# The pool scale repeated by its load, a new order of early loads, and copies and norms exchanged at two changes of stage

## The chip, the cores and the metric

The kernel runs on one core of a Trainium2 chip. The metric is the device time of one execution in microseconds (us). Engines are named as the profile names them: PE (TensorE, matmuls), PEld (its weight loads), DVE (VectorE), ACT (ScalarE), POOL (GpSimd) and SP (SyncE, which issues most loads and stores). A name with a q (SPq, ACTq) is the engine's instruction queue, where DMAs are issued.

## The reference

A two-layer decoder trunk over 512 tokens of 1024 channels. The parts that matter here:

```python
def rms_norm(x, g):
    y = x * rsqrt(mean(x * x, axis=-1) + 1e-6)
    return y * g

def pool_mixer(h, w_pool, scale):          # layer 0
    # 4 channel groups of 256; group g: causal trailing mean over 2, 4, 8, 16 tokens, minus the token
    d = stack(diffs)                       # (B, S, 4, 256)
    y = einsum('bsgc,gcd->bsgd', d, w_pool).reshape(B, S, D)
    return y * scale                       # per output channel

x = x + rms_norm(pool_mixer(rms_norm(x, mix_pre_g[0]), pool_w[0], pool_scale[0]), mix_post_g[0])
x = x + rms_norm(conv_glu_ffn(rms_norm(x, ffn_pre_g[0]), ...), ffn_post_g[0])
# shared K/V from rms_norm(x, kv_norm_g); then layer 1:
x = x + rms_norm(sliding_window_attention(rms_norm(x, mix_pre_g[1]), K, V, sinks) @ w_o, mix_post_g[1])
x = x + rms_norm(conv_glu_ffn(rms_norm(x, ffn_pre_g[1]), ...), ffn_post_g[1])
```

`conv_glu_ffn` multiplies by `w_in` (1024 to 5632), convolves over three tokens, takes gelu(gate) * value and multiplies by `w_out` (2816 to 1024).

## The kernel before

The 512 tokens are four blocks of 128 (`x0` to `x3`, tokens on the partitions). Products of the large matmuls are split in two: each operand is a rounded high part and the remainder (`h`/`l`), and `mm3` issues three matmuls for one product (L319 high x high, L320 and L321 the mixed ones). So each operand costs a copy on ACT (the high part) and a subtraction on DVE (the low part).

The order of the work on PE, ACT, DVE and POOL is the order in which the program emits it; nothing reorders these four. SP's DMAs are placed by the tile framework, which also adds the waits: a tile with the same tag as another takes its buffer, and what writes it waits for the last access of the tile that had it. The eight PSUM banks are such buffers (`bank`), handed out in turn.

**Start.** PE first runs 13 matmuls on a constant tile (`keep_busy`, L346). x0 comes in two halves (L96). `mix_norm` (L356) squares x on ACT, takes the root on POOL and scales on DVE. `mix_pool` (L386 to 392) applies the pooling matrices `band` (its last 128 columns for block 0, the others for blocks 1 to 3) with matmuls in full precision and copies the result `d` on ACT. `mix_map` (L401) multiplies `d` by the weights `wp`. These are made by `mix_weights` (L375) on DVE: pool weights x pre-norm gain x pool scale. The scale is one row of 1024 numbers, but it is wanted on all 128 partitions: it is loaded into partition 0 of a zeroed tile (L87, L329), split into two parts (`mix_row`, L363 to L365), and repeated over the partitions by four matmuls with a matrix of ones into two PSUM banks (L371). After it come the post-norm (L281, L283), the pre-norm of the FFN (L304) and the transposes (`transpose_in`: PE L312, ACT L315, DVE L316) into `xT`, which the FFN multiplies (`u`, L319 to L321).

**Early loads.** x0, `band`'s last part, the scale row, the constants, the pool weights (1 MB), x2, a gain row, x3 and the first FFN weights go through SP's queue in that order; x1 and `band`'s first part through ACT's. Gain rows are loaded repeated over the partitions (`bcast_row`, L245). The scale row and the gain rows share a tag with two buffers ("bc").

**First FFN to attention.** `pass2` ends the FFN. Its last sums are formed as `X[3]` and `X[2]` on PE; `add`, `square_of`, `gain`, `root` and `update` (L665, L251, L687, L259/L260, L696) then make the post-norm and the new x. Blocks 2 and 3 are ready early: their pre-norm (`pre_a`: squares and root, `pre_b`: scaling) and their transposes (`to_attention`) stand between the matmuls. Blocks 0 and 1 follow after the last matmuls. Attention begins with the keys of blocks 2 and 3 (`kp`), their values (`vp`), and the transposes and keys of blocks 0 and 1.

**Attention to second FFN.** Per block b the output projection (`op`, two halves), the post-norm and the pre-norm are emitted (L1057 to L1067); the transposes of blocks 0 and 1 stand in between, those of 2 and 3 inside `start1`, which runs the first two units of `w_in` on two blocks at a time: `yield j, (b0, b1)` is unit j for blocks b0 to b1-1, with both its halves (gate and value).

**Tail.** In layer 1 `update` also stores x; the last are blocks 0 and 1.

Of the kernel before, what the change touches and what calls it, by code (L numbers as in the profile page):

```python
# [8 lines left out]
F32 = mybir.dt.float32  # L9
F32R = mybir.dt.float32r  # L10
# [5 lines left out]
P = 128  # L16
S = 512
D = 1024
# [53 lines left out]
def build(nc, tc, ctx, a, out):  # L72
# [7 lines left out]
    def bank(name):  # L80
        return ps.tile([P, 512], F32, tag="ps", name=name)
# [1 line left out]

    warm = pc.tile([P, P], F32, tag="t4", name="warm", bufs=3)
    nc.vector.memset(warm, 1.0)
    row = pc.tile([P, D], F32, tag="bc", name="row", bufs=2)
    nc.vector.memset(row, 0.0)  # L87
    x = [pc.tile([P, D], F32, tag="x", name=f"x{b}", bufs=4) for b in range(NB)]
    def new_xT(name):
        h = pc.tile([P, NB, KC, P], F32R, tag="xTh", name=f"xTh_{name}")  # L90
# [43 lines left out]
    def source(i):  # L134

        for l in range(2):
            if U_D1[l] <= i < U_D2[l]:
                p = i - U_D1[l]
                return 2048, [(0, a["ws"][W_OUT[l] + p][:, 0:512]), (512, sums[l][p][:, :])]
            if U_D2[l] <= i < U_D3[l]:  # L140
                m = i - U_D2[l]
                n = min(NP - 4 * m, 4) * 512
                return n, [(0, sums4[l][m][:, 0:n])]
            if U_D3[l] <= i < U_D3[l] + 6:
                m = i - U_D3[l]
                q = range(2 * m, min(2 * m + 2, NP))
                return len(q) * 1024, [((p % 2) * 1024, a["ws"][W_OUT[l] + p][:, 1024:2048]) for p in q]
        return 2048, [(0, a["ws"][i if i < U_D1[0] else i + W_SHIFT])]

    def load(i):  # L150
        if i in raws or i in ready or i >= N_UNITS:
            return
        r = pw.tile([P, 2048], F32, tag="raw", name=f"raw{i}", bufs=2)
        for o, src in source(i)[1]:
            nc.sync.dma_start(r[:, o : o + src.shape[1]], src)
        raws[i] = r
# [81 lines left out]
    def ahead(i, n=N_SLOTS):  # L238

        for k in range(i, i + n):  # L240
            split(k)
# [65 lines left out]
    def transpose_in(b, xn, xT, name):  # L307
        for h in range(2):
            pt = bank(f"tr_{name}{b}{h}")
            for k in range(4):  # L310
                kc = h * 4 + k
                nc.tensor.transpose(pt[:, k * P : (k + 1) * P], xn[:, kc * P : (kc + 1) * P], ident)  # L312
            hi = xT[0][:, b, h * 4 : (h + 1) * 4, :].rearrange("p k t -> p (k t)")
            lo = xT[1][:, b, h * 4 : (h + 1) * 4, :].rearrange("p k t -> p (k t)")
            nc.scalar.copy(hi, pt)  # L315
            nc.vector.tensor_tensor(lo, pt, hi.bitcast(F32), ALU.subtract)  # L316
# [9 lines left out]
    nc.scalar.dma_start(x[1], a["x"][1])  # L326
    nc.scalar.dma_start(band[:, :, : P + EDGE], a["band"][:, :, : P + EDGE])
    nc.sync.dma_start(band[:, :, P + EDGE :], a["band"][:, :, P + EDGE :])
    nc.sync.dma_start(row[0:1], a["pool_scale"])  # L329
    nc.sync.dma_start(cst[:, :C_LATE], a["cst"][:, :C_LATE])  # L330
    load(U_POOL)
    nc.sync.dma_start(x[2], a["x"][2])
    post_row = bcast_row(a["mix_post_g"][0], "mpost0")
# [6 lines left out]
    scale_row = [bank(f"scale_row{h}") for h in range(2)]  # L340
    scratch = bank("scratch")

    def keep_busy(n):
# [12 lines left out]
            nc.vector.tensor_scalar(halves(xm)[h], halves(x[b])[h], r, None, ALU.mult)  # L356
        xns[b] = xm

    parts = [pm.tile([P, D], F32R, tag=f"row{i}", name=f"row{i}") for i in range(2)]
    one = pm.tile([P, P], F32R, tag="one", name="one")  # L360

    def mix_row():
        nc.vector.tensor_copy(one, warm)  # L363
        nc.scalar.copy(parts[0], row)
        nc.vector.tensor_tensor(parts[1], row, parts[0].bitcast(F32), ALU.subtract)  # L365

    def mix_weights():

        for h in range(2):
            for i in range(2):  # L370
                nc.tensor.matmul(scale_row[h], one, parts[i][:, h * 512 : (h + 1) * 512], start=i == 0, stop=i == 1)  # L371
        pr = raws[U_POOL]
        for c in range(8):
            g = c // 2
            nc.vector.scalar_tensor_tensor(wp[:, c, :], pr[:, c * 256 : (c + 1) * 256], gain_col(0, c),  # L375
                                           scale_row[g // 2][:, (g % 2) * 256 : (g % 2 + 1) * 256], ALU.mult, ALU.mult)

    def mix_pool(b):
        d = pm.tile([P, D], F32, tag="d", name=f"d{b}", bufs=2)
# [32 lines left out]

    u0, u1 = U_IN[0], U_IN[0] + 1
    mix_norm(0)
    mix_row()
    mix_norm(1)
    d0 = mix_pool(0)
    mix_weights()
# [206 lines left out]
    def pass2(l, p2, G2, X, post_row):  # L625
# [32 lines left out]
        def soon(k):  # L658
            if k < len(todo):
                n, m = todo[k]  # L660
                split((U_D2 if n == 2 else U_D3)[l] + m)
                split2(n, m)

        def add(z, i, q):
            nc.vector.tensor_tensor(Z[z][i], Z[z][i], X[q][i], ALU.add)  # L665
# [12 lines left out]
        def square_of(z, i, q):  # L678

            b = i + (2 if z[0] == "2" else 0)  # L680
            first = b not in ss
            if first:
                ss[b] = new_ss(f"p_f{l}{b}")
            square(X[q][i], Z[z][i], ss[b], int(z[1]) - 1, first)

        def gain(z, i):
            nc.vector.tensor_tensor(Z[z][i], Z[z][i], gains[int(z[1]) - 1], ALU.mult)  # L687

        def root(b):
            rs[b] = rstd_end(ss[b])  # L690

        def update(b):
            r = rs[b]
            for h in range(2):
                xs = halves(x[b])[h]
                nc.vector.scalar_tensor_tensor(xs, Z[f"{b // 2 + 1}{h + 1}"][b % 2], r, xs, ALU.mult, ALU.add)  # L696
# [27 lines left out]
        for p in range(NP - NT):  # L724
            for q in of:
                make(q, p, (0, 1))
            if p == 0:
                for i in range(2):
                    add("21", i, 4)
                    square_of("21", i, 4)  # L730
                    root(2 + i)
                soon(5)
                for i in range(2):
                    gain("21", i)
                soon(6)
                for i in range(2):
                    update(2 + i)
            if p == 2:
                then(pre_a, 2)
                then(pre_b, 2)  # L740
                soon(7)
                then(pre_a, 3)
                then(pre_b, 3)
            if p == 5:
                soon(8)
                then(split, U_K)
            if p == 7:
                then(split, U_V)
                then(to_attention, 2)

        for i in range(2):
            for q in of:
                for p in range(NP - NT, NP):
                    make(q, p, (i,))
                if i == 0 and q == 3:
                    then(to_attention, 3)
        add("12", 0, 3)
        square_of("12", 0, 3)
        add("11", 0, 2)
        square_of("11", 0, 2)  # L760
        root(0)
        gain("12", 0)
        gain("11", 0)
        add("12", 1, 3)
        square_of("12", 1, 3)
        update(0)
        add("11", 1, 2)
        square_of("11", 1, 2)
        root(1)
        gain("12", 1)  # L770
        gain("11", 1)
        then(pre_a, 0)
        update(1)
        then(pre_b, 0)
# [17 lines left out]
    with tc.tile_pool(name="att", bufs=1, reuse_waits="tile") as pa:  # L792
# [264 lines left out]
        for b in range(NB):  # L1057
            if b < 2:
                split(U_IN[1] + b)
            o_proj(1, b, os[1, b], (0,))  # L1060
            if b == 3:
                transpose_in(1, xnf[1], xT, "f1")
            o_proj(1, b, os[1, b], (1,))
            if b == 2:
                transpose_in(0, xnf[0], xT, "f1")
            post_norm(b, acc[b], post_row, "m1", pa)
            xnf[b] = pre_norm(b, pre_row, "f1")  # L1067

    def start1():
        yield 0, (0, 2)  # L1070
        transpose_in(2, xnf[2], xT, "f1")
        yield 1, (0, 2)
        transpose_in(3, xnf[3], xT, "f1")
        ahead(U_IN[1])
        yield 0, (2, 4)
        yield 1, (2, 4)
# [86 lines left out]
```

## Time and profile before

| | |
|---|---|
| median of 3 runs | 928.75 us (lowest 928.23) |
| profiled execution | 929.28 us, span 927.5 us |
| mean granted clock of TensorE | 0.996 |
| busy, share of the span | PE 98%, PEld 84%, DVE 70%, ACT 50%, POOL 34% |
| moved by DMA | 178.5 MB, 192 GB/s over the span |

Times in the profile count from the start of the span. A timeline row gives start and duration in us, engine, line of the kernel, operation, output <- inputs, shape and the number of instructions merged into the row; in brackets stands how long the engine had been idle and what ended that. A row of the waits says for which instruction an engine waited, for whom, how many us in total, how often, and the longest. The chain is followed back from the last instruction: at each step to what released it.

### The profile page before, as it was taken

The page shows a single profiled execution, that of the slowest core. Times are in us where ns is not written, and L with a number is a line of the kernel's source. Part 1 is how long each engine was busy: PE and PEld are TensorE (multiplying, and loading weights), DVE is VectorE, ACT ScalarE, POOL GpSimd, SP SyncE. Part 2 cuts the span into 40 slices and gives each one's busy share as a digit, 9 for nine tenths or more (in the row PEclk, how much of TensorE's full clock was granted, in tenths as well). Part 3 has the DMA queues.
Part 4 walks back from the last instruction along what each step waited for, and adds up shares of the span by engine and source line. Part 5 has one row for each costly group of instructions (what it writes and reads, how often), then busy time and mean ns, then how long its engine had stood idle before and what let it go on. Part 6 is the DMA issues. An engine that isn't in the chain of part 4 may idle for free.

```text
span 927.5 us, 12780 instructions
## 1 busy us (share of the span) xinstructions
PE 908.5 (98%) x4702; PEld 778.2 (84%) x4702; DVE 652.3 (70%) x956; ACT 467.2 (50%) x816; POOL 317.7 (34%) x373
## 2 busy tenths in 40 slices
PE   8999999999999999999999999999999999999996
PEld 8998888888887878799899888988888888888785
DVE  4878867776677787944999836565555555677877
ACT  5745444445444665554788634433344333455562
POOL 2424444444341000235657212344444333410001
PEclk9999999999999999999999999999999999999999
DMA  8266797878884664831112243355555555456643
GB/s 309 104 215 217 282 314 265 295 279 304 269 292 140 207 215 167 319 147 48 46 46 93 88 161 139 137 189 210 200 185 205 201 196 186 161 163 202 222 168 113
DMA packets 45040, 178.49 MB, mean 192 GB/s; under 512 B 5297, under 2 KB 6833, under 8 KB 36658
## 3 DMA queue, kind: packets, MB, share of 16 engines
q1 hardware_dynamic: 42578, 164.28, 50.5%
q10 hardware_dynamic: 2400, 13.40, 3.7%
q8 instruction: 37, 0.61, 0.3%
q14 instruction: 25, 0.20, 0.1%
HBM read 139.91 MB, written 37.75 MB: 192 GB/s over the span
## 4 chain that ended last, share of the span: by engine, by line
PE 81%; DVE 9%; POOL 3%; issue 3%; ACT 2%; DMA 1%; POOLq 0%; DVEq 0%; ACTq 0%; SPq 0%
PE u L320 17%; PE u L321 16%; PE u L319 16%; PE dn L320 5%; PE dn L321 5%; PE dn L319 5%; DVE wl L233 2%; PE op L319 1%; PE op L321 1%; PE op L320 1%; DVE P L907 1%; PE qp L319 1%; PE qp L321 1%; PE qp L320 1%; PE pT L915 1%
## 5 line engine op out<-in xcount | busy, mean ns | idle before, releaser
L320 PE MATMUL u<-xTl_f,wh 128*128 128x512 f32 (+1 forms) x768 | 285.4, 372 | 2.0 <-DVE xTl_f L316 2.0
L319 PE MATMUL u<-xTh_f,wh 128*128 128x512 f32 (+1 forms) x768 | 285.7, 372 | 0.2 <-ACT xTh_f L315 0.2
L321 PE MATMUL u<-xTh_f,wl 128*128 128x512 f32 (+1 forms) x768 | 285.2, 371 | 0.0
L233 DVE TENSOR_TENSOR wl<-raw,wh 128x1024 fp32r<-128x1024 f32 (+1 forms) x158 | 206.0, 1344 | 13.3 <-ACT wh L232 13.2
L320 PEld LDWEIGHTS u<-xTl_f,wh 128*128 128x128 f32 x768 | 144.7, 188 | 27.2 <-DVE xTl_f L316 2.5
L536 DVE SCALAR_TENSOR_TENSOR t<-u,conv,t 128x511 f32<-128x511 f32 x88 | 65.8, 747 | 144.1 <-ACT t L535 144.1
L319 PEld LDWEIGHTS u<-xTh_f,wh 128*128 128x128 f32 x768 | 144.7, 188 | 25.6 <-ACT xTh_f L315 0.5
L321 PEld LDWEIGHTS u<-xTh_f,wl 128*128 128x128 f32 x768 | 144.7, 188 | 24.9
L232 ACT CAST wh<-raw 128x1024 fp32r<-128x1024 f32 (+1 forms) x158 | 156.8, 1041 | 9.0 <-DMA raw<-t 6.1
L535 ACT ACTIVATE t<-u,conv 128x512 f32<-128x512 f32 x88 | 68.3, 777 | 137.3 <-PE u L321 103.2
L556 POOL TENSOR_TENSOR G<-G,G 128x256 f32<-128x256 f32 x22 | 33.0, 1501 | 270.3 <-DVE G L551 270.3
L320 PE MATMUL dn<-wl,gh 128*128 128x512 f32 x276 | 108.0, 391 | 3.1 <-DVE wl L233 3.1
L319 PE MATMUL dn<-wh,gh 128*128 128x512 f32 x276 | 107.6, 390 | 0.0
L321 PE MATMUL dn<-wh,gl 128*128 128x512 f32 x276 | 107.5, 390 | 0.1
L544 ACT ACTIVATE t<-t 128x512 f32<-128x512 f32 x44 | 27.8, 633 | 104.3 <-DVE t L537 104.3
L537 DVE SCALAR_TENSOR_TENSOR t<-u,conv,t 128x510 f32<-128x510 f32 x88 | 65.9, 749 | 3.1
L320 PEld LDWEIGHTS dn<-wl,gh 128*128 128x128 f32 x276 | 51.8, 188 | 15.6 <-DVE wl L233 5.1
L321 PEld LDWEIGHTS dn<-wh,gl 128*128 128x128 f32 x276 | 51.8, 188 | 11.1 <-DVE gl L650 0.6
L319 PEld LDWEIGHTS dn<-wh,gh 128*128 128x128 f32 x276 | 51.8, 188 | 10.8
L253 POOL TENSOR_SCALAR ss_p_f<-ss_p_f 128x1 f32<-128x1 f32 x8 | 3.3, 419 | 159.4 <-ACT dn L251 159.4
L577 ACT CAST gh<-G 128x1024 fp32r<-128x1024 f32 x22 | 23.1, 1050 | 56.6 <-DVE G L575 42.2
L578 DVE TENSOR_TENSOR gl<-G,gh 128x1024 fp32r<-128x1024 f32 x22 | 27.5, 1250 | 26.9 <-ACT gh L577 19.9
(198 smaller groups left out, 1529.9 us busy)
## 6 DMA issues: line engine op xcount, KB each, us to landing
raw<-in_ws_dram SPq DMA_DIRECT2D x49, 1024.0 KB, 5.0
q<-in_ws_dram SPq DMA_DIRECT2D x44, 512.0 KB, 6.5
raw<-t SPq DMA_DIRECT2D x24, 768.0 KB, 5.5
t<-q SPq DMA_DIRECT2D x44, 256.0 KB, 2.9
t<-q SPq DMA_DIRECT2D x22, 512.0 KB, 3.0
raw<-in_ws_dram SPq DMA_DIRECT2D x22, 512.0 KB, 4.6
r<-in_ws_dram SPq DMA_DIRECT2D x12, 512.0 KB, 6.7
hi<-h SPq DMA_DIRECT2D x12, 512.0 KB, 5.9
```

The costliest lines, as they stand in the source:

```text
L232: nc.scalar.copy(hi[:, s], r[:, s])
L233: nc.vector.tensor_tensor(lo[:, s], r[:, s], hi[:, s].bitcast(F32), ALU.subtract)
L319: nc.tensor.matmul(acc, ah, bh, start=first, stop=False)
L320: nc.tensor.matmul(acc, ah, bl, start=False, stop=False)
L321: nc.tensor.matmul(acc, al, bh, start=False, stop=last)
L535: nc.scalar.activation(t, u, AF.Identity, bias=conv_col(l, ch, 3), scale=conv_col(l, ch, 2))
L536: nc.vector.scalar_tensor_tensor(t[:, 1:], u[:, : S - 1], conv_col(l, ch, 1), t[:, 1:], ALU.mult, ALU.add)
L537: nc.vector.scalar_tensor_tensor(t[:, 2:], u[:, : S - 2], conv_col(l, ch, 0), t[:, 2:], ALU.mult, ALU.add)
L544: nc.scalar.activation(tg, tg, AF.Gelu_apprx_tanh)
L556: nc.gpsimd.tensor_tensor(s1, s1, G2[:, p, 2, :], ALU.add)
L577: nc.scalar.copy(h, G1[:, o : o + 1024])
L578: nc.vector.tensor_tensor(lo, G1[:, o : o + 1024], h.bitcast(F32), ALU.subtract)
```

## The change

1. The pool scale is loaded repeated over the partitions into an SBUF tile (`scale_row`, tag "bc"). The zeroed row, `mix_row` with its two parts and the tile of ones, the four matmuls and their two PSUM banks go. `mix_weights` reads the SBUF tile.
2. Early loads: x1 and `band`'s first part move from ACT's queue to SP's, `band`'s last part from SP's to ACT's; the order on SP becomes x0, x1, constants, first part of `band`, scale, pool weights. The pool weights come in two halves of 1024 columns.
3. End of the first FFN: the scaling `pre_b(3)` is emitted three pairs later, behind the weight split `soon(8)`; the transposes of block 3 stand behind the last `q == 2` matmuls for i = 0, not behind `q == 3`.
4. End of the second FFN (layer 1 only): `gain` writes to an unused part of `Z2` instead of in place, directly after its `add` and `square_of`; `gain("12", 1)` comes ahead of `add("11", 1)`. In layer 0 the order of these calls stays.
5. Attention to second FFN: the pre-norm of block 2 is emitted in the step of block 3, behind the transposes of block 1. The transposes of block 3 stand between the two halves of unit 1, not behind them.

```diff
-    row = pc.tile([P, D], F32, tag="bc", name="row", bufs=2)
-    nc.vector.memset(row, 0.0)
+    scale_row = pc.tile([P, D], F32, tag="bc", name="scale_row", bufs=2)
...
+        ws = a["ws"][i if i < U_D1[0] else i + W_SHIFT]
+        if i == U_POOL:
+            return 2048, [(o, ws[:, o : o + 1024]) for o in (0, 1024)]
+        return 2048, [(0, ws)]
...
-    nc.scalar.dma_start(x[1], a["x"][1])
-    nc.scalar.dma_start(band[:, :, : P + EDGE], a["band"][:, :, : P + EDGE])
-    nc.sync.dma_start(band[:, :, P + EDGE :], a["band"][:, :, P + EDGE :])
-    nc.sync.dma_start(row[0:1], a["pool_scale"])
+    nc.scalar.dma_start(band[:, :, P + EDGE :], a["band"][:, :, P + EDGE :])
+    nc.sync.dma_start(x[1], a["x"][1])
     nc.sync.dma_start(cst[:, :C_LATE], a["cst"][:, :C_LATE])
+    nc.sync.dma_start(band[:, :, : P + EDGE], a["band"][:, :, : P + EDGE])
+    nc.sync.dma_start(scale_row, a["pool_scale"][0].partition_broadcast(P))
     load(U_POOL)
...
-    def mix_row():
-        nc.vector.tensor_copy(one, warm)
-        nc.scalar.copy(parts[0], row)
-        nc.vector.tensor_tensor(parts[1], row, parts[0].bitcast(F32), ALU.subtract)
...
-        for h in range(2):
-            for i in range(2):
-                nc.tensor.matmul(scale_row[h], one, parts[i][:, h * 512 : (h + 1) * 512], start=i == 0, stop=i == 1)
...
-                                           scale_row[g // 2][:, (g % 2) * 256 : (g % 2 + 1) * 256], ALU.mult, ALU.mult)
+                                           scale_row[:, g * 256 : (g + 1) * 256], ALU.mult, ALU.mult)
...
+        Y = {(z, i): Z2[:, (4 + k) * 512 : (5 + k) * 512]
+             for k, (z, i) in enumerate((z, i) for z in ("11", "12") for i in range(2)) if l == 1}
+
         def gain(z, i):
-            nc.vector.tensor_tensor(Z[z][i], Z[z][i], gains[int(z[1]) - 1], ALU.mult)
+            nc.vector.tensor_tensor(Y.get((z, i), Z[z][i]), Z[z][i], gains[int(z[1]) - 1], ALU.mult)
...
-                nc.vector.scalar_tensor_tensor(xs, Z[f"{b // 2 + 1}{h + 1}"][b % 2], r, xs, ALU.mult, ALU.add)
+                z = f"{b // 2 + 1}{h + 1}", b % 2
+                nc.vector.scalar_tensor_tensor(xs, Y.get(z, Z[z[0]][z[1]]), r, xs, ALU.mult, ALU.add)
...
                 then(pre_a, 3)
-                then(pre_b, 3)
             if p == 5:
                 soon(8)
+                then(pre_b, 3)
                 then(split, U_K)
...
-                if i == 0 and q == 3:
+                if i == 0 and q == 2:
                     then(to_attention, 3)
-        add("12", 0, 3)
...
+        for i in range(2):
+            add("12", i, 3)
+            square_of("12", i, 3)
+            if i:
+                update(0)
+            if l:
+                gain("12", i)
+            add("11", i, 2)
+            square_of("11", i, 2)
+            if l:
+                gain("11", i)
+            root(i)
+            if not l:
+                gain("12", i)
+                gain("11", i)
         then(pre_a, 0)
...
                 transpose_in(1, xnf[1], xT, "f1")
+                xnf[2] = pre_norm(2, pre_row, "f1")
             o_proj(1, b, os[1, b], (1,))
...
-            xnf[b] = pre_norm(b, pre_row, "f1")
+            if b != 2:
+                xnf[b] = pre_norm(b, pre_row, "f1")
...
-        yield 1, (0, 2)
+        yield 1, (0, 2), (0,)
         transpose_in(3, xnf[3], xT, "f1")
+        yield 1, (0, 2), (1,)
         ahead(U_IN[1])
```

More of the change, by code (lines that the diff above doesn't have):

```diff
@@ L147, in source @@
                 return len(q) * 1024, [((p % 2) * 1024, a["ws"][W_OUT[l] + p][:, 1024:2048]) for p in q]
-        return 2048, [(0, a["ws"][i if i < U_D1[0] else i + W_SHIFT])]
+        ws = a["ws"][i if i < U_D1[0] else i + W_SHIFT]
+        if i == U_POOL:
+            return 2048, [(o, ws[:, o : o + 1024]) for o in (0, 1024)]
+        return 2048, [(0, ws)]
     def load(i):
@@ L339, in build @@
     load_conv(0)
-    scale_row = [bank(f"scale_row{h}") for h in range(2)]
     scratch = bank("scratch")
@@ L357, in mix_norm @@
         xns[b] = xm
-    parts = [pm.tile([P, D], F32R, tag=f"row{i}", name=f"row{i}") for i in range(2)]
-    one = pm.tile([P, P], F32R, tag="one", name="one")
-    def mix_row():
-        nc.vector.tensor_copy(one, warm)
-        nc.scalar.copy(parts[0], row)
-        nc.vector.tensor_tensor(parts[1], row, parts[0].bitcast(F32), ALU.subtract)
     def mix_weights():
-        for h in range(2):
-            for i in range(2):
-                nc.tensor.matmul(scale_row[h], one, parts[i][:, h * 512 : (h + 1) * 512], start=i == 0, stop=i == 1)
         pr = raws[U_POOL]
@@ L414, in build @@
     mix_norm(0)
-    mix_row()
     mix_norm(1)
@@ L754, in pass2 @@
                     make(q, p, (i,))
-                if i == 0 and q == 3:
+                if i == 0 and q == 2:
                     then(to_attention, 3)
-        add("12", 0, 3)
[L758 to L771, printed above, removed]
+        for i in range(2):
[13 more added lines that the diff above has]
+                gain("11", i)
         then(pre_a, 0)
```

## The prediction

> **What bounds the kernel now.** I read the page first, then the waits of PE, then the chain of waits over the first 20 us, then the timelines of the three places that the change touches.
>
> ```profile
> span 927.5 us, 12780 instructions
> PE 908.5 (98%) x4702; PEld 778.2 (84%) x4702; DVE 652.3 (70%) x956; ACT 467.2 (50%) x816; POOL 317.7 (34%) x373
> ```
>
> PE is busy for 98% of the span, so only what PE idles, what it does needlessly, and the tail can be won: 927.5 - 908.5 = 19 us in all. The waits of PE say where (us in total, times, longest):
>
> ```profile
> PE pd L388 <- DVE xm L356: 2.1, 1, 2.1
> PE u L320 <- DVE xTl_f L316: 2.0, 2, 1.6
> PE tr_f L312 <- DVE xn_f L304: 0.9, 1, 0.9
> PE u L319 <- ACT xTh_f L315: 0.2, 1, 0.2
> ```
>
> The first and third lie in the pool mixer at the start; the second and fourth at the change from attention to the second FFN. The change works on these two places, on the change from the first FFN to attention (where PE shows no wait at all), and on the tail. I sum the four places one by one.
>
> **1. The start.** The chain, in order of time (start, us, what), and the other engines:
>
> ```profile
> 8.39 3.46 PE pd L388 x16
> 11.85 1.16 PE scale_row L371 x4
> ...
> 16.48 3.56 PE my L401 x16
> ```
>
> ```profile
> 0.86 0.37 ACTq L326 DMA_DIRECT2D x<-in_x_dram  x1
> 4.10 0.63 ACT L251 ACTIVATE xm<-x 128x512 f32<-128x512 f32 x1 [1.88 <-DMA x<-in_x_dram]
> 6.11 0.63 ACT L251 ACTIVATE xm<-x 128x512 f32<-128x512 f32 x1 [1.29 <-DMA x<-in_x_dram]
> 7.85 0.88 DVE L356 TENSOR_SCALAR xm<-x,ss_m 128x512 f32<-128x512 f32 x2 [5.79 <-POOL ss_m L260]
> 12.58 3.22 DVE L375 SCALAR_TENSOR_TENSOR wp<-raw,cst,scale_row 128x256 f32<-128x256 f32 x8 [0.65 <-PE scale_row L371]
> 4.09 0.33 SPq L332 DMA_DIRECT2D x<-in_x_dram  x1
> 5.38 0.33 SPq L245 DMA_DIRECT2D mpost<-in_mix_post_g_dram  x1
> 10.03 0.33 SPq L245 DMA_DIRECT2D fpre<-in_ffn_pre_g_dram  x1
> 25.53 1.41 DVE L304 SCALAR_TENSOR_TENSOR xn_f<-x,ss_n_f,fpre 128x512 f32<-128x512 f32 x2 [0.73 <-POOL ss_n_f L260]
> ```
>
> PE is the chain from 8.39 on; it started there because the second half of x0 landed at 6.1, 2.3 us earlier. Removed are the four scale_row matmuls (1.16 us of the chain), the DVE memset, cast and subtraction, and the ACT cast. Only the matmuls lay on the path.
>
> *x0.* Now x0 (524 KB) shares the engines with x1 (524 KB on ACT's queue). Afterwards only 262 KB of the band run beside it. So at least 262 KB fewer are ahead of x0's end, at most 524 + 295 - 262 = 557 KB; at the 361 GB/s quoted below that is 0.7 to 1.5 us. ACT's first square (4.10 + 0.72 with its accumulator read) ends at 4.8 and limits the gain to 1.3 us. I take 1.2: PE starts at 7.2, bounds 7.1 to 7.7.
>
> *The clock.* Columns: stretch, its length, busy time of PE, PEld, DVE, ACT, POOL, granted clock, DMA share, GB/s.
>
> ```profile
> 4.00:6.00 2.00, 2.00 (x14) 2.00 (x13) 0.00 (x0) 0.72 (x2) 0.22 (x1) 1.00 1.05 361
> 8.50:9.00 0.50, 0.50 (x4) 0.50 (x5) 0.50 (x3) 0.50 (x3) 0.20 (x1) 0.78 0.91 377
> 11.50:12.00 0.50, 0.50 (x3) 0.48 (x3) 0.43 (x2) 0.12 (x1) 0.00 (x0) 0.50 0.94 254
> 12.00:12.50 0.50, 0.50 (x3) 0.37 (x2) 0.00 (x0) 0.50 (x2) 0.00 (x0) 0.80 0.92 320
> 570.00:575.00 5.00, 4.52 (x37) 4.52 (x38) 3.54 (x6) 1.34 (x4) 1.21 (x4) 1.00 0.37 77
> ```
>
> After the wait of 2.1 us the clock was 0.50 from about 8.8 to 12.2, so pd0 took 3.46/16 = 0.216 us a pass; my0 at full clock takes 3.56/16 = 0.22 us for 256 columns, half as much a column. A wait of 1.6 us elsewhere (the row at 570) left the clock at 1.00. With PE at work until 6.3 and again from 7.2 the wait is 0.9 us, and I take the clock as staying full: pd0 then lasts 16 x 0.11 = 1.8 and ends at 9.0. [...]
>
> *x1, band, weights.* Issues with KB and median us to landing:
>
> ```profile
> x<-in_x_dram SPq DMA_DIRECT2D x2, 512.0 KB, 8.0
> x<-in_x_dram ACTq DMA_DIRECT2D x1, 512.0 KB, 4.5
> mpost<-in_mix_post_g_dram SPq DMA_DIRECT2D x1, 512.0 KB, 7.7
> ```
>
> x1 landed at 0.86 + 4.5 = 5.4. Moved to SP's queue behind x0, it comes 524/361 = 1.5 us after x0, at about 6.4; a chain like x0's (2.3 us, and 0.7 for the other half's square) puts xm1 at 9.4. pd1 starts there and lasts as now, 16.48 - 11.85 - 1.16 = 3.5, to 12.9. The weights: x2 lands now at 4.09 + 8.0 = 12.1, with 3.26 MB issued up to its end. In the new order 2.73 MB stand up to the end of the pool's first half, the broadcast row's 524 KB included: 0.53 MB less at 377 GB/s, so 10.7, and 12.1 for the second half. The products (3.22/8 = 0.40 us) run 10.7 to 12.3 and 12.3 to 13.9. my0 needs the last of them only 2.7 us after its start, at 15.6. So my0 starts at 12.9 instead of 16.48: **-3.6 us**. What follows my0 (its squares, the root, the update of x0, the next norm) hangs on it and moves with it; the 0.9 us wait at tr_f stays.
>
> What the new traffic can delay: x2 comes 0.52 MB or 1.4 us later, at 13.5, so ACT's two squares of x2 (0.7 each) hold d1's two copies, behind them in ACT's order, until 14.9; done at 15.9, and my1 wants d1 at 16.5 (12.9 + 3.56). That is the thinnest cover, 0.6 us. mpost goes from 5.38 + 7.7 = 13.1 to 14.5; it is wanted when the first half of my0 is squared, at 12.9 + 1.8 + 0.7 = 15.4. scale_row now holds its "bc" buffer until the last product, so fpre is issued at 13.9 instead of 10.03; behind it on SP stands only the second W_in unit, which also waits for the products. With mpost's 7.7 us it lands at 21.6, and the first pre-norm wants it at 25.53 - 3.6 = 21.9; the queue ahead of it is shorter by then than ahead of mpost, so I cost this at nothing, and at up to 1 us if the landing takes longer. Bounds of the place: -1.2 (the matmuls gone, nothing earlier) to -4.2 (x1 so early that pd1 follows pd0 at 9.0, and x0 0.1 earlier still).
>
> **2. First FFN to attention.**
>
> ```profile
> 386.34 1.03 PE L312 MATMUL tr_a<-cst,xn_a 128*128 128x128 f32 x8
> 387.59 1.29 DVE L316 TENSOR_TENSOR xTl_a<-tr_a,xTh_a 128x512 fp32r<-128x512 f32 x2 [0.45 <-ACT xTh_a L315]
> 393.72 0.68 DVE L665 TENSOR_TENSOR Z<-Z,dn 128x512 f32<-128x512 f32 x1
> 394.43 0.60 ACT L251 ACTIVATE dn<-Z 128x512 f32<-128x512 f32 x1 [1.43 <-DVE Z L665]
> 396.23 0.28 PE L319 MATMUL kp<-wh,xTh_a 128*128 128x256 f32 x1
> 406.13 1.29 DVE L316 TENSOR_TENSOR xTl_a<-tr_a,xTh_a 128x512 fp32r<-128x512 f32 x2 [0.17 <-ACT xTh_a L315]
> 407.41 0.36 PE L319 MATMUL kp<-wh,xTh_a 128*128 128x256 f32 x1
> ```
>
> The transposes of block 3 go behind nine more matmuls (9 x 0.23 = 2.0 us on PE), and PE's total is unchanged. But their two DVE subtractions stand ahead of all the final additions in DVE's order. They move from 387.59 to 389.6, and add("12",0), the squares, gains, update(0) and add("11",1) move with them, as the row at 393.72 shows no idle time before it: it becomes about 395.7. Two things on PE wait for that chain. The second kp (396.23) takes the PSUM bank that the square at 394.43 releases at 395.1: 0.9 us late. kp of block 0 (407.41) needs the first half of xTl_a, ready at 406.13 + 0.6 = 406.75, so it had 0.7 us of slack; the chain before it (pre_a, pre_b, kst, V, xTh on ACT) is late by 2.0. Cost 2.0 - 0.7 = 1.3, less 0.1 for the first matmuls, which need only xTh: **+1.2 us**; bounds 0 (PE shows no wait there now) and +2.0 (no slack at all). pre_b(3) behind soon(8) lets DVE split weights first; since PE waits for neither, that is nothing, and the transposes want pre_b(3) only 2.0 us later than now.
>
> **3. Attention to second FFN.**
>
> ```profile
> 568.41 1.41 DVE L304 SCALAR_TENSOR_TENSOR xn_f<-x,ss_n_f,fpre 128x512 f32<-128x512 f32 x2 [1.77 <-POOL ss_n_f L260]
> 569.75 1.28 DVE L316 TENSOR_TENSOR xTl_f<-tr_f,xTh_f 128x512 fp32r<-128x512 f32 x2
> ```
>
> xTl_f of block 1 stood behind the norm of block 2, which waited 1.77 us for POOL. In the new order it starts when DVE ends update of block 2, at 568.41 - 1.77 = 566.6, and ends at 567.8. PE's wait ended with the first half, at 569.75 + 0.6 = 570.4, and so began at 568.8: the 1.6 us go. The norm of block 2 comes 0.6 us later, to 570.4, and is wanted by transposes behind a whole half unit (48 matmuls of 0.12 us, 574.5). The transposes of block 3 a half unit earlier (24 matmuls, 2.9 us) take the other 0.4 + 0.2 us: together **-2.2 us**, bounds -1.6 and -2.3.
>
> **4. The tail.**
>
> ```profile
> 918.72 1.41 DVE L696 SCALAR_TENSOR_TENSOR x<-Z,ss_p_f,x 128x512 f32<-128x512 f32 x2
> 922.94 1.41 DVE L696 SCALAR_TENSOR_TENSOR x<-Z,ss_p_f,x 128x512 f32<-128x512 f32 x2 [0.73 <-POOL ss_p_f L260]
> 920.65 0.69 DVE L687 TENSOR_TENSOR Z<-Z,fpost 128x512 f32<-128x512 f32 x1
> 564.35 0.20 POOL L259 TENSOR_TENSOR ss_p_m<-ss_p_m 128x1 f32<-128x1 f32 x1 [0.42 <-ACT pt_m L251]
> 921.63 0.63 POOL L259 TENSOR_TENSOR ss_p_f<-ss_p_f 128x1 f32<-128x1 f32 x1 [1.42 <-ACT dn L251]
> ```
>
> Writing the gained rows elsewhere frees gain of the wait for the squares. But gain("12",1), 0.6 of its 0.69 us, now stands before add("11",1) and delays the last sum of squares. In return no gain runs beside POOL's last sum, which takes 0.63 beside one and 0.20 at 564.35 without one: 0.4 us back. update(0) gains 0.2 in the same way. Sum **0**, bounds -0.6 (add not delayed) and +0.6 (POOL no faster).
>
> **Sum.** -3.6 + 1.2 - 2.2 + 0 = -4.6. The profiled execution took 929.28, which would become 924.7; the median of the runs is 928.75, 0.5 lower, and I forecast such a median: 924.1.
>
> **Rivals.** *Half clock again.* [...] pd0 is then mostly through by 8.8; pd1 runs at half pace from 9.4 to 12.2, does 1.4 us of its 3.5, and ends at 14.3: -2.2 at the start, sum -3.2, 925.5. Chance 0.20.
>
> *The copies at place 2 cost nothing*, if ACT's chain has more slack than I see: -5.8, 922.9. For it: PE shows no wait there. Against: 0.7 us of slack. Chance 0.10.
>
> *The loads do not come earlier*, the queues being served otherwise than I think; only the matmuls leave: -1.2 + 1.2 - 2.2 = -2.2, 926.6. Chance 0.14.
>
> *Slower: the broadcast row holds up SP's queue.* 128 reads of one 4 KB row may run below the rate. Places 2 to 4 give -1.0, so it decides where my0 starts after 17.5, with the pool's first half at 16.7, 6.0 us later than reckoned: 524 KB in 7.4 us, 71 GB/s. At half of that the row takes 14.8 us, my0 starts at 24.9 instead of 16.5, and the sum is +7.4: 936.2. Against: mpost is a row repeated in the same way and landed 13.1 - 12.1 = 1.0 us behind x2. Chance 0.03.
>
> **Numbers.** The forecast has 0.53, with a range of its own of 923 to 925. 922.0 to 927.2 holds all cases but the slower one, with 0.5 us at each end for what runs of the kernel before differ (928.23, 928.75), and leaves out 0.15. Two per cent (910 to 947, about what a measurement of this kernel tells from no change) is beyond every case: within 0.97, faster 0.01, slower 0.02.
>
> **What would show it.** pd L388 from 7.2 at granted clock 1.00; no scale_row; my at 12.9; a late second kp and a new PE wait for xTl_a of about 0.4 behind it; u no longer waiting for xTl_f; the last L696 4.2 to 4.4 us after the one before it (now 922.94 - 918.72 = 4.2). I am wrong if my0 starts after 14.5, if add("11",1) follows PE's last product as now, or if PE waits elsewhere.

## The result, and the profile after

The changed kernel takes 923.36 us (median of 5 runs) where the kernel before takes 928.75: a ratio of 0.9945, with a 95% interval of 0.9931 to 0.9959. A second comparison gave 0.9951 (0.9938 to 0.9963). That is 4.6 to 5.1 us less, below the two per cent that count as a difference and inside the range; the forecast was 924.1. The sum came out, but two of its four terms did not, and an edit that I had costed at nothing was worth 1.5 us. The first profiled execution of the changed kernel ran at a granted clock of 0.65 and 1310 us, so what follows is read from the second comparison's, which took 923.77 us. Its lines have other numbers than before: pd0 is L377 (before L388), pd1 L379 and L380, `my` L390 (L401).

The page, after:

```profile
span 922.0 us, 12766 instructions
PE 906.7 (98%) x4698; PEld 776.5 (84%) x4698; DVE 650.3 (71%) x953; ACT 465.9 (51%) x815; POOL 319.4 (35%) x373
```

PE has four matmuls and 1.8 us less to do, and the span is 5.5 us shorter: most of it is idle time that went. The waits of PE, after (us in total, times, longest):

```profile
PE dn L322 <- DVE wl L235: 1.8, 3, 0.7
PE pd L377 <- DVE xm L357: 1.5, 1, 1.5
...
PE tr_f L314 <- DVE xn_f L306: 0.9, 1, 0.9
...
PE kt L827 <- ACT kst L821: 0.3, 1, 0.3
PE pd L379 <- DVE xm L357: 0.2, 1, 0.2
PE kp L323 <- DVE xTl_a L318: 0.2, 1, 0.2
```

The waits of `u` for `xTl_f` and `xTh_f` are gone, and `kt` and `kp` have new ones. The first line had a counterpart before that the prediction did not look at:

```profile
PE dn L320 <- DVE wl L233: 3.1, 4, 1.3
```

The start, after, from the timeline:

```profile
1.04 5.81 PE L347 MATMUL scratch<-warm 128*128 128x128 f32 x26 [1.04 <-DVE warm L85]
3.51 0.63 ACT L253 ACTIVATE xm<-x 128x512 f32<-128x512 f32 x1 [1.29 <-DMA x<-in_x_dram]
6.04 0.63 ACT L253 ACTIVATE xm<-x 128x512 f32<-128x512 f32 x1 [1.81 <-DMA x<-in_x_dram]
7.71 0.63 ACT L253 ACTIVATE xm<-x 128x512 f32<-128x512 f32 x1 [0.94 <-DMA x<-in_x_dram]
8.33 2.05 PE L377 MATMUL pd<-band,xm 128*128 128x128 f32 x16 [1.48 <-DVE xm L357]
10.61 0.49 PE L379 MATMUL pd<-band,xm 128*128 128x128 f32 x2 [0.23 <-DVE xm L357]
11.37 3.25 DVE L364 SCALAR_TENSOR_TENSOR wp<-raw,cst,scale_row 128x256 f32<-128x256 f32 x8 [0.43 <-DMA raw<-in_ws_dram]
14.20 4.13 PE L390 MATMUL my<-wp,d 128*128 128x256 f32 x18
```

The ACT rows are the squares that follow the two halves of x0 and the landing of x1. x0's second half is squared at 6.04, about as before (6.11), so pd0 starts at 8.33 and not at the 7.2 that I forecast; x1 lands at 7.7, not at 6.4; my0 starts at 14.20, not at 12.9. Two other profiles with the same loads (the start alone and the transposes back, both below) have x0's second half at 5.74 and 5.41 and x1 at 7.65 and 7.50: x0 differs from run to run, x1 hardly.

**The stretches.** Starts of PE rows in each profile give the table that the rest argues from: the first `my` and the first `u` matmul of the kernel, from there to the first `kp` (the first FFN), from there to the first `qp` (keys and values), and the granted clock while pd0 runs. The next two columns are kernels that the experiments below define.

| us | before | after | scale alone | copies alone | pre_b alone |
|---|---|---|---|---|---|
| first `my` | 16.33 | 14.20 | 13.67 | 16.34 | 15.12 |
| first `u` | 40.13 | 37.99 | 37.48 | 40.13 | 38.92 |
| clock at pd0 | 0.5 | 1.0 | 1.0 | 0.5 | 1.0 |
| `u` to `kp` | 353.23 | 351.76 | 352.98 | 351.66 | 351.90 |
| `kp` to `qp` | 25.64 | 26.64 | 25.65 | 26.64 | 25.64 |

### The profile page after: what moved, and what is told of

Its sections match the earlier page's. It is cut to its first block, busy times and chain, and to the rows that moved or that the text cites. A ratio compares the mean times of both kernels' runs of the same rounds, so it can differ in the third digit from the quotient of the medians.

```text
span 1308.5 us, 12766 instructions
## 1 busy us (share of the span) xinstructions
PE 1299.0 (99%) x4698; PEld 911.8 (70%) x4698; DVE 653.8 (50%) x953; ACT 470.7 (36%) x815; POOL 312.1 (24%) x373
## 4 chain that ended last, share of the span: by engine, by line
PE 99%; DMA 0%; DVE 0%; ACT 0%; POOL 0%; issue 0%; DVEq 0%; POOLq 0%; SPq 0%; ACTq 0%
PE u L321 18%; PE u L322 18%; PE u L323 18%; PE dn L322 8%; PE dn L323 8%; PE dn L321 8%; PE my L390 2%; PE op L323 2%; PE qp L321 2%; PE op L321 2%; PE qp L323 2%; PE qp L322 2%; PE op L322 2%; PE pT L909 1%; PE pd L379 1%; PE tr_f L314 1%
## 5 line engine op out<-in xcount | busy, mean ns | idle before, releaser
L321 PE MATMUL u<-xTh_f,wh 128*128 128x512 f32 (+1 forms) x768 | 370.4, 482 | 0.0
L322 PE MATMUL u<-xTl_f,wh 128*128 128x512 f32 (+1 forms) x768 | 369.6, 481 | 0.0
L323 PE MATMUL u<-xTh_f,wl 128*128 128x512 f32 (+1 forms) x768 | 369.4, 481 | 0.0
L322 PEld LDWEIGHTS u<-xTl_f,wh 128*128 128x128 f32 x768 | 165.5, 215 | 76.4 <-issue 25.8
L323 PEld LDWEIGHTS u<-xTh_f,wl 128*128 128x128 f32 x768 | 165.5, 215 | 76.2 <-issue 25.8
L321 PEld LDWEIGHTS u<-xTh_f,wh 128*128 128x128 f32 x768 | 165.2, 215 | 76.4 <-issue 25.7
L321 PE MATMUL dn<-wh,gh 128*128 128x512 f32 x276 | 140.2, 508 | 0.0
L323 PE MATMUL dn<-wh,gl 128*128 128x512 f32 x276 | 140.0, 507 | 0.0
L322 PE MATMUL dn<-wl,gh 128*128 128x512 f32 x276 | 140.0, 507 | 0.0
L323 PEld LDWEIGHTS dn<-wh,gl 128*128 128x128 f32 x276 | 57.2, 207 | 32.8 <-issue 11.0
```

Of the source, the lines that this page charges most:

```text
L321: nc.tensor.matmul(acc, ah, bh, start=first, stop=False)
L322: nc.tensor.matmul(acc, ah, bl, start=False, stop=False)
L323: nc.tensor.matmul(acc, al, bh, start=False, stop=last)
```

## The experiments

Every ratio is to the kernel before on the same chip, with its 95% interval; 0.001 is 0.93 us.

**The whole change again.** No edit.

> The whole change again, for its trace. By the prediction's sum: my0 starts at 12.9 (before 16.48), a late second kp and about 1.2 us lost between the first FFN and attention, no wait of u for xTl_f, the last update 4.2 to 4.4 us after the one before it; time 4.6 us under the kernel before. If the copies between the first FFN and attention cost nothing: 5.8 under, with no new wait of PE. If the clock halves again: 3.2 under, granted clock 0.50 between 9 and 12.

Measured: 924.43 us against 929.08, 0.9951 (0.9938 to 0.9963); its profile is shown above.

**The start alone.** The kernel before with the new loads and the scale by its load (items 1 and 2 of the change).

```diff
+    nc.scalar.dma_start(band[:, :, P + EDGE :], a["band"][:, :, P + EDGE :])
+    nc.sync.dma_start(x[1], a["x"][1])
+    nc.sync.dma_start(scale_row, a["pool_scale"][0].partition_broadcast(P))
```

> Only the start changed: the new order of loads and the scale repeated by its load. Prediction: -3.6 us (clock full, my0 at 12.9). Half clock again: -2.2. Loads not earlier, only the matmuls gone: -1.2. A broadcast row that holds up the queue: slower.

Measured: 0.9986 (0.9977 to 0.9995), some 1.3 us instead of 3.6. In its profile pd0 runs at half clock all the same:

```profile
8.02 3.68 PE L378 MATMUL pd<-band,xm 128*128 128x128 f32 x16 [2.09 <-DVE xm L357]
15.03 3.27 PE L391 MATMUL my<-wp,d 128*128 128x256 f32 x14
```

The first `u` starts at 38.83. At the same half clock it was 40.13 before: the edit is worth 1.3 us, close to the 1.2 that the rival "only the matmuls leave" gives.

**The copies at place 2 alone** (item 3, both of its moves).

```diff
-                then(pre_b, 3)
             if p == 5:
                 soon(8)
+                then(pre_b, 3)
...
-                if i == 0 and q == 3:
+                if i == 0 and q == 2:
                     then(to_attention, 3)
```

> Only the first FFN's end changed: pre_b(3) behind soon(8), the transposes of block 3 behind the last q == 2 matmuls. Prediction: +1.2 us, with the second kp late by 0.9 and kp of block 0 waiting for xTl_a. Rival: 0.0 us, no wait.

Measured: 0.9997 (0.9989 to 1.0006), no loss where I had +1.2. The table says why: the stretch from `kp` to `qp` is 1.00 us longer, but that from `u` to `kp` is 1.57 shorter. The second is the other move, which stands alone below.

**The change from attention to the second FFN alone** (item 5).

```diff
+                xnf[2] = pre_norm(2, pre_row, "f1")
...
-        yield 1, (0, 2)
+        yield 1, (0, 2), (0,)
         transpose_in(3, xnf[3], xT, "f1")
+        yield 1, (0, 2), (1,)
```

> Only the change from attention to the second FFN: the norm of block 2 behind the transposes of block 1, those of block 3 between the halves of unit 1. Prediction: -2.2 us, the three waits of u (1.6, 0.4, 0.2) gone. Rival (the norm of block 2, 0.6 us later, makes its transposes wait): -1.6.

Measured: 0.9969 (0.9958 to 0.9979), 2.9 us, more than the 2.3 that I gave as the bound. The timelines of the kernel before and of this one, from the first `u` of the second FFN to ACT's first read of a finished `u`:

```profile
568.58 0.28 PE L319 MATMUL u<-xTh_f,wh 128*128 128x256 f32 x1
570.48 0.39 PE L320 MATMUL u<-xTl_f,wh 128*128 128x256 f32 x1 [1.63 <-DVE xTl_f L316]
587.89 0.78 ACT L535 ACTIVATE t<-u,conv 128x512 f32<-128x512 f32 x1 [1.46 <-PE u L321]
```

```profile
567.23 0.28 PE L319 MATMUL u<-xTh_f,wh 128*128 128x256 f32 x1
567.34 0.28 PE L320 MATMUL u<-xTl_f,wh 128*128 128x256 f32 x1
583.54 0.78 ACT L535 ACTIVATE t<-u,conv 128x512 f32<-128x512 f32 x1 [3.22 <-PE u L321]
```

19.31 us became 16.31. The wait at 570.48 is listed with 1.63, counted from the modelled end of the matmul before it, which is 0.28 long; but such matmuls follow each other at 0.12. From start to start 1.90 us lie between two that now stand 0.11 apart, so the stall was 1.8. The same reading of the other two waits gives 0.6 and 0.5: 2.9 of the 3.0 us, where the view lists 2.2. This kernel leaves the start as it was, and still its pd0 ran at full clock after a longer gap than the kernel before had (2.65 us, against 2.13 with 0.50):

```profile
1.04 4.64 PE L346 MATMUL scratch<-warm 128*128 128x128 f32 x26 [1.04 <-DVE warm L85]
8.33 2.05 PE L388 MATMUL pd<-band,xm 128*128 128x128 f32 x16 [2.65 <-DVE xm L356]
```

So in these two profiles the longer gap kept the clock: its length alone does not sort them. The kernel with a longer warm-up, below, goes on from here.

**pre_b(3) alone.**

```diff
                 then(pre_a, 3)
-                then(pre_b, 3)
             if p == 5:
                 soon(8)
+                then(pre_b, 3)
```

> The kernel before with one step moved: pre_b(3) behind soon(8); the transposes of block 3 stay. New theory: PE lost 1.3 us because the split of the last output weights waited in DVE's order behind pre_b(3), which waited for POOL; then kp starts 1.3 to 1.6 us earlier and the time falls by as much. The prediction's step (PE waits for neither): 0.0.

Measured: 0.9981 (0.9972 to 0.9990), 1.8 us from a move that I had costed at nothing. The timeline of the kernel before shows it:

```profile
383.33 0.88 DVE L297 TENSOR_SCALAR xn_a<-x,ss_n_a 128x512 f32<-128x512 f32 x2 [0.72 <-POOL ss_n_a L260]
384.12 1.22 DVE L233 TENSOR_TENSOR wl<-raw,wh 128x1024 fp32r<-128x1024 f32 x1
385.40 0.50 PE L320 MATMUL dn<-wl,gh 128*128 128x512 f32 x1 [1.32 <-DVE wl L233]
```

DVE waits 0.72 us for POOL's root and scales block 3 for 0.8 more, and the split of the last weights, which PE needs at once, stands behind that. With the norm moved, PE has no wait left between 376 and 420 us. The prediction read no row of this stretch before it said that "PE waits for neither"; the page's list had the wait in its total of 3.1 us, and I had not asked for it by window.

**A longer warm-up.** The kernel before, with more matmuls ahead of the first load's landing, so that PE idles less before pd0.

```diff
-    keep_busy(13)
+    keep_busy(20)
```

> The kernel before with keep_busy(20) for keep_busy(13), which only closes PE's gap ahead of pd0 (from 2.1 to about 0.5 us). If the length of the gap decides the clock, as predicted: clock 1.00 from 8 to 14 in every execution, pd0 in 2.0 us, time -1.4 against executions with the half clock. [...]

Measured: 0.9994 (0.9985 to 1.0003). In its profile the gap is 1.11 us and pd0 runs at 1.00. All 11 executions have a mean granted clock of 0.997 to 0.999, and spans that average 926.85 us. The kernel before had 0.994 to 0.996 in 19 of its 33 runs beside these (928.1 us in the mean) and 0.997 or 0.998 in 14 (926.75). In the profiles of all the experiments, the four that lost a stretch to half clock have means of 0.993 to 0.997 and the nine others 0.997 to 0.999, so I read 0.996 or less as a stretch lost, while a rounded 0.997 can be either. So half clock at pd0 is a matter of the run for the kernel before, it costs some 1.4 us, and with the gap shortened none of 11 runs has a mean that low, while the full-clock case gets no shorter.

**The tail alone** (item 4).

```diff
-            nc.vector.tensor_tensor(Z[z][i], Z[z][i], gains[int(z[1]) - 1], ALU.mult)
+            nc.vector.tensor_tensor(Y.get((z, i), Z[z][i]), Z[z][i], gains[int(z[1]) - 1], ALU.mult)
```

> Only the tail: gained rows written elsewhere, gain(12,1) ahead of add(11,1). Prediction: 0.0, the last update 4.2 to 4.4 us after the one before it. If POOL's faster sum outweighs: -0.4. If the later add outweighs: +0.6.

Measured: 1.0005 (0.9995 to 1.0014): nothing. The timeline of the whole change shows both halves of the trade:

```profile
914.43 0.68 DVE L680 TENSOR_TENSOR Z<-Z,fpost 128x512 f32<-128x512 f32 x1
915.03 0.68 DVE L653 TENSOR_TENSOR Z<-Z,dn 128x512 f32<-128x512 f32 x1
916.62 0.19 POOL L261 TENSOR_TENSOR ss_p_f<-ss_p_f 128x1 f32<-128x1 f32 x1 [2.03 <-ACT dn L253]
917.49 1.42 DVE L690 SCALAR_TENSOR_TENSOR x<-Z,ss_p_f,x 128x512 f32<-128x512 f32 x2 [1.05 <-POOL ss_p_f L262]
```

The gain at 914.43 holds the last addition back, and POOL's sum takes 0.19 where it took 0.63. PE's last product starts 3.37 us before the last update, 3.46 before the change.

**x0 with nothing beside it.** The changed kernel with `band`'s last part on SP's queue behind x0, so that ACT's queue is empty.

```diff
-    nc.scalar.dma_start(band[:, :, P + EDGE :], a["band"][:, :, P + EDGE :])
+    nc.sync.dma_start(band[:, :, P + EDGE :], a["band"][:, :, P + EDGE :])
     nc.sync.dma_start(x[1], a["x"][1])
```

> The changed kernel, but the last part of band is issued by SP behind x0, so nothing stands beside x0. If what runs beside x0 sets its landing (the prediction's step): the second half lands 0.7 us before 6.0, pd0 starts at about 7.6, time 0.5 under the changed kernel. If later loads of the same queue overtake it: 6.0 again, no change.

Measured: 0.9986 (0.9972 to 1.0001), 928.38 us: 0.0035 or 3.3 us behind the changed kernel (0.9951). The timeline of this kernel:

```profile
6.45 2.05 PE L377 MATMUL pd<-band,xm 128*128 128x128 f32 x16 [0.31 <-DVE xm L357]
10.67 0.49 PE L379 MATMUL pd<-band,xm 128*128 128x128 f32 x2 [2.17 <-DVE xm L357]
16.39 2.06 PE L390 MATMUL my<-wp,d 128*128 128x256 f32 x4
```

And two of its stretches (stretch, length, busy time of PE, PEld, DVE, ACT, POOL, granted clock, DMA share, GB/s):

```profile
14.00:16.00 2.00, 2.00 (x10) 2.00 (x11) 1.15 (x3) 1.67 (x5) 0.41 (x2) 0.50 1.06 436
...
18.00:20.00 2.00, 2.00 (x9) 1.68 (x8) 0.00 (x0) 0.43 (x1) 0.00 (x0) 0.81 1.04 393
```

x0's second half is squared at 4.17 instead of 6.04, so `band`'s 262 KB on the other queue cost it 1.9 us, and pd0 starts at 6.45 at full clock. But x1 still lands at 7.8, pd1 starts at 10.67, as in the changed kernel (10.61), and the time that pd0 no longer fills has become a gap of 2.17 us behind it. The clock falls to 0.50 from 12 to nearly 19 us, and the first `u` starts at 41.35, 3.4 us later than after the change. Neither expectation had this: x0 came 1.9 us earlier where 0.7 was expected, and the time went up. The cost goes with the clock: the two of the ten executions with a mean clock of 0.998 or more have spans of 922.5 and 923.5 us, like the changed kernel, and the other eight (0.992 to 0.995) 925.4 to 929.5. An earlier x0 is worth nothing while x1 decides, and it can cost.

**Transposes of block 3 back.** The changed kernel, with `pre_b(3)` left where it was moved.

```diff
-                if i == 0 and q == 2:
+                if i == 0 and q == 3:
                     then(to_attention, 3)
```

> The changed kernel with the transposes of block 3 back behind the q == 3 matmuls; pre_b(3) stays moved. New theory (the moved transposes cost 1.0 us, because their subtractions hold the final additions): no wait of kt and kp, 1.0 us under the changed kernel, 6.0 under the kernel before. Rival (the cost was only a difference of two uncertain times): the same as the changed kernel.

Measured: 923.09 us, 0.9933 (0.9921 to 0.9945): the lowest median of all. From `kp` to `qp` it takes 25.66 us instead of 26.64, and the waits of `kt` and `kp` are gone. That the move costs 1.0 us is thus shown in both directions, on the kernel before and on the one after, and in every other profile too: 26.63 to 26.65 us with the transposes moved, 25.64 to 25.66 without. The timed difference to the changed kernel (0.9951) is the right way, but the intervals touch. The two profiled spans differ by only 0.4 us, because in this profile the first FFN (`u` to `kp`) took 352.80 us, 1.0 more than the changed kernel's, with 0.7 us of waits of `dn` for `gl` that the other does not have.

**Both x first.** The changed kernel with x0 and x1 first on SP's queue and both parts of `band` behind them; ACT's queue is empty.

```diff
-    nc.scalar.dma_start(band[:, :, P + EDGE :], a["band"][:, :, P + EDGE :])
     nc.sync.dma_start(x[1], a["x"][1])
-    nc.sync.dma_start(cst[:, :C_LATE], a["cst"][:, :C_LATE])
+    nc.sync.dma_start(band[:, :, P + EDGE :], a["band"][:, :, P + EDGE :])
     nc.sync.dma_start(band[:, :, : P + EDGE], a["band"][:, :, : P + EDGE])
+    nc.sync.dma_start(cst[:, :C_LATE], a["cst"][:, :C_LATE])
```

> The changed kernel with x0 and x1 first on SP's queue, then both parts of band, then the constants; nothing on ACT's queue. If the 512-byte pieces of band hold up what runs beside and behind them: x0 whole at about 4.1, x1 at 5.5 (now 7.7), pd0 at about 7, my0 at 12.2 (now 14.2), time 1 to 2 us under the changed kernel. Rival (the rate is low then whatever the order): x1 at 7, my0 at 13.5 or later, within 0.7 of the changed kernel.

Measured: 924.18 us, 0.9946 (0.9935 to 0.9958), no difference from the change. Its timeline:

```profile
6.84 0.63 ACT L253 ACTIVATE xm<-x 128x512 f32<-128x512 f32 x1 [1.74 <-DMA x<-in_x_dram]
7.77 2.02 PE L377 MATMUL pd<-band,xm 128*128 128x128 f32 x16 [2.12 <-DMA band<-in_band_dram]
9.75 0.49 PE L379 MATMUL pd<-band,xm 128*128 128x128 f32 x2
12.17 3.25 DVE L364 SCALAR_TENSOR_TENSOR wp<-raw,cst,scale_row 128x256 f32<-128x256 f32 x8 [2.08 <-DMA raw<-in_ws_dram]
```

x1 lands 0.9 us earlier, pd1 follows pd0 without a gap, and my0 starts at 13.34, 0.86 earlier. Of this 0.55 is left at the first `u` (37.44), and in this profile the first FFN gave it back (352.49 us from `u` to `kp`, with 0.5 us of waits of `dn` for `gl` that the changed kernel's profile does not have). pd0 now waits for `band`, and the pool weights come 0.8 later. The rival's numbers (x1 at 7, my0 at 13.5) are the nearer ones. From 2 to 4 us 269 GB/s moved, against 331 in the kernel before, though both parts of `band` are issued behind x0 and x1 here (at 2.11 and 2.81 us). That the small pieces make the rate low at first is not shown; why it is low stays open.

**Transposes back, x first, and the tail's gain swapped.** The two edits above together, and `gain("12", 1)` behind `add("11", 1)`.

```diff
-            if l:
+            if l and not i:
                 gain("12", i)
             add("11", i, 2)
             square_of("11", i, 2)
+            if l and i:
+                gain("12", i)
             if l:
                 gain("11", i)
```

> Both of the other edits of the changed kernel, and gain(12,1) behind add(11,1) again in the tail: 2.0 to 3.0 us under the changed kernel if both theories hold, about 7 under the kernel before; the last part alone 0.0 to -0.4.

Measured: 923.62 us, 0.9935 (0.9922 to 0.9947). That is 5.8 us under the kernel before, where about 7 was expected. Its profiled span is the shortest (920.5), with 3.05 us from PE's last product to the last update. But the runs do not tell it from the kernel with the transposes alone (0.9933), so the load order and the tail's order are worth too little to be measured here.

**The scale alone.** The kernel before with item 1 only; the loads in their old order and the pool weights in one piece.

```diff
-    nc.sync.dma_start(row[0:1], a["pool_scale"])
+    nc.sync.dma_start(scale_row, a["pool_scale"][0].partition_broadcast(P))
...
-                nc.tensor.matmul(scale_row[h], one, parts[i][:, h * 512 : (h + 1) * 512], start=i == 0, stop=i == 1)
```

> The kernel before with the scale repeated by its load and the four matmuls gone; the order and queues of the other loads as before, the pool weights in one piece. If the new order of loads gains nothing: -1.2, as the whole start. If it gains: under half of that. If the 512 KB of the row hold up the weights here, my0 waits for them: 0.0.

Measured: 0.9992 (0.9983 to 1.0001). The timed gain is too small to be sized, but the profile is plain: my0 starts at 13.67 at full clock, earlier than in the changed kernel.

```profile
6.01 0.63 ACT L250 ACTIVATE xm<-x 128x512 f32<-128x512 f32 x1 [1.22 <-DMA x<-in_x_dram]
8.29 2.05 PE L375 MATMUL pd<-band,xm 128*128 128x128 f32 x16 [2.62 <-DVE xm L354]
13.67 4.56 PE L388 MATMUL my<-wp,d 128*128 128x256 f32 x20
```

Four of the kernels above keep the old loads and the old scale and had full clock in their profiles (attention alone, `pre_b` alone, the longer warm-up, the tail alone): they reach the first `u` at 38.91 to 39.00. With the scale alone it is 37.48, with the scale and the new loads 37.99 (37.80 with the transposes back), with both x first 37.44. In these profiles the gain at the start, about 1.4 us, is all from the scale's matmuls and copies; the new order of loads gives nothing, and as changed it takes 0.3 to 0.5 back. The timed ratios (0.9992 here, 0.9986 for the start alone) cannot tell the two apart.

## Why the prediction was right, and where it was wrong

**In total** the forecast was 924.1 and the runs gave 923.4 and 924.4. In the two profiles the terms are these; the first column is the sum on record.

| | forecast | profiles | what it was |
|---|---|---|---|
| start | -3.6 | -2.1 | -1.0 at one clock, the rest the clock of these two runs |
| first FFN, `pre_b(3)` | 0 | -1.5 | a wait of PE that I had not seen |
| transposes of block 3 | +1.2 | +1.0 | the size as argued, the waits in part |
| attention to second FFN | -2.2 | -3.0 | the waits, measured from start to start |
| tail | 0 | -0.1 | as argued |
| attention itself | | +0.2 | unexplained |
| sum | -4.6 | -5.5 | spans: 922.0 - 927.5 = -5.5 |

Errors of 1.5 us at the start one way, and of 1.5 at `pre_b(3)` and 0.8 at the attention the other way, stand in it: that the total was met is luck in part. Without the clock's share of 1.1 the sum is -4.4. The runs beside each other agree: at a mean granted clock of 0.997 or more the kernel before has spans of 926.5 us (mean of 11) and the changed one 922.3 (mean of 4), 4.2 less.

**The start: the step that failed is the landing of x1 "at about 6.4"** (7.5 to 7.7 in three profiles), and with it x0's 1.2 us (0.1 to 0.7). From x1's square to my0 the forecast needs 6.5 us (6.4 to 12.9). The changed kernel takes 14.20 - 7.71 = 6.5, the kernel with both x first 13.34 - 6.84 = 6.5. So that chain is right, and only the landing was mis-sized. I divided the bytes ahead by the 361 GB/s of the kernel before. These are the stretches after the change, with the GB/s last:

```profile
2.00:4.00 2.00, 2.00 (x12) 2.00 (x11) 0.00 (x0) 0.70 (x2) 0.00 (x0) 1.00 0.92 271
4.00:6.00 2.00, 2.00 (x11) 2.00 (x11) 0.00 (x0) 0.23 (x2) 0.22 (x1) 1.00 0.94 302
6.00:8.00 2.00, 0.85 (x5) 0.65 (x4) 0.22 (x1) 1.02 (x3) 0.75 (x2) 1.00 1.08 328
```

From 4 to 6 us the rate is 302 and not 361 (267 and 278 in the two other profiles with these loads). And 271 x 2 + 302 x 2 + 328 x 1.7 is 1.70 MB up to 7.7 us, where x0, x1 and `band`'s last part are 1.31 MB: loads queued behind x1 already take their share. The rival "the loads do not come earlier, only the matmuls leave" (-1.2, chance 0.14) describes the start: -1.0 at one clock. The covers that I named held: from the first `my` to the first `u` it is 23.8 us before and after, so mpost, fpre and d1's copies delayed nothing.

**The clock: the conclusion held in most runs, the reason was half of it.** In the changed kernel's profile pd0 ran at 1.00 after a gap of 1.48 us. But it also did after 2.62, 2.65 and 2.77 us in kernels that load x0 in the old way, and ran at 0.50 after 2.13 (before), 1.98 (copies alone) and 2.09 (start alone). The kernel with both x first had 1.00 after 2.12 us, practically the gap of the kernel before. What goes with the outcome is the length of the warm-up: the same 26 matmuls take 4.60 to 4.64 us in the profiles that kept full clock through a gap of 2.1 us or more, and 4.89 to 5.41 in the three that lost it; gaps of 1.8 us or less ahead of pd0 (warm-ups of 4.97 to 5.81) lost nothing there.

So the gaps that pd0 kept full clock through are 0.31 to 1.78 us and 2.12 to 2.77 us long, and those with which it lost it 1.98 to 2.13 us: the lengths overlap. The half clock did not last equally long either: from 8.78 to 12.20 us in the kernel before, and from 12 to nearly 19 us with nothing beside x0, though PE was busy all through that (2.00 of every 2.00 us from 12 to 20). What decides it is not shown; no kernel here was made to vary the length of the warm-up with the gap held.

Nor does the change make the gap short every time: the same start gave 1.48, 1.69 and 2.09 us in three profiles. In the experiments 43 of 73 runs of the kernel before have a mean clock of 0.996 or less, and 3 of 21 with the new start (the changed kernel, the start alone, the transposes back). So the stretch at half clock became rarer and did not go.

**The first FFN: the step that failed is "since PE waits for neither, that is nothing".** PE waited 1.32 us for exactly that split. With the norm moved, the stretch from `u` to `kp` shrank by 1.5 us in one pair of profiles. The move was a gain in its own right (0.9981).

**The transposes: right in sign and size** (+1.0 for +1.2), and in the waits only in part. `kp` of block 0 waits for `xTl_a` (0.2), as expected, and `kt` for `kst` (0.3), which the forecast had in the chain ahead of it. But the "late second kp" did not come: it starts 2.87 us after the first, before and after the change, though after the change the square that should have held its bank starts later than that, at 3.02. My rival that this costs nothing (0.10) is out.

**Attention to the second FFN: the mechanism right, the size of the waits wrong** (-3.0 for -2.2): the list of waits counts from modelled ends.

**The tail: right.** Updates 917.49 - 913.11 = 4.4 us apart, as forecast, with the two effects that were set against each other.

## What to carry to other kernels

Ask for the waits window by window at every place that a change touches, also where it only reorders: a wait of 1.3 us hid in a line that was a sum over the whole span. Where two loads run at once, size a landing from a run in which they do, and ask which of two inputs lands last before moving the other forward: an early first stage only opens a gap behind it. And separate the edits even when the total fits, because one part of this change cost a microsecond that the others hid; without it the kernel has the lowest median of those tried, 923.09 us, 0.9933 (0.9921 to 0.9945) of the time before, in an interval that touches the changed kernel's.

## What the runs showed of the hardware that I had not expected

- A gap on PE of about 2 us was followed by a stretch at half clock in some profiles and by none in others (0.50 after 2.13 us, 1.00 after 2.12); what decides it is not shown. The kernel before had a mean granted clock of 0.996 or less in 19 of 33 runs and was 1.4 us longer in these; a gap of 2.17 us was followed by nearly 7 us at half clock once (12 to 19 us with nothing beside x0).
- With 262 KB on the second queue x0's second half was squared at 5.41 to 6.04 us (three profiles), without them at 4.17 to 4.46 (three others).
- A stall of PE among matmuls that follow each other at 0.12 us was listed 0.16 us short of what it cost (1.63 listed, 1.79 lost).
- The first FFN itself is not equally long from run to run: with the norm in its old place, 352.98 to 354.09 us from `u` to `kp` in six profiles, and with it moved, 351.66 to 352.80 in seven. The waits that the view lists account for a part of this only. Terms of less than a microsecond are not to be read from one pair of profiles there.
